# A float32 decoder trunk on one core: in the gate and up product, two of eight pairs of feature tiles are multiplied blockwise with seven products (Strassen's scheme) instead of eight

## The chip, the core and the metric

The kernel runs on one core of a Trainium2 chip. The core has TensorE (matrix products, called PE in the profile; its weight loads, PEld, are listed apart and overlap the products), VectorE (DVE), ScalarE (ACT), GpSimd (POOL) and SyncE (SP, which here only issues transfers). The metric is the device time of one execution in microseconds (us).

## The reference, cut to what matters

One sequence of 256 tokens with 2048 features goes through two layers: dilated attention and then attention over a shared latent K/V, each followed by this feed-forward part with 5632 hidden features:

```python
def swiglu(xn, w_gu, w_down):
    g, u = jnp.split(xn @ w_gu, 2, axis=-1)
    return (jax.nn.silu(g) * u) @ w_down

h = h + swiglu(rms_norm(h, ffn_norm_g[layer]), ffn_w_gu[layer], ffn_w_down[layer])
```

`xn` is 256 x 2048, `w_gu` is 2048 x 11264 (gate columns, then up columns), `w_down` is 5632 x 2048. Everything is float32.

## The kernel before, in words

**Precision.** A float32 operand is split into two parts, `hi` (rounded to the format that TensorE multiplies in one pass, fp32r) and `lo` (the rest). A product of two such operands is three matmuls, hi·hi, hi·lo and lo·hi, added up in PSUM (lines 416 to 418). So one 128-token tile by one 128 x 512 weight block costs three matmuls of 512 columns.

**Weights.** All weights come as units of 128 partitions x 2048 values, in one list made in advance. `WeightStream` (lines 84 to 158) loads a unit from HBM into one of four `raw` buffers (line 100, on SP's queue), and splits it in two halves of 1024: ACT copies `hi` (line 141), DVE subtracts to get `lo` (line 142). `hi` and `lo` have three buffers each (`ahead + 1`), so the split of a unit can begin when PE is done with the unit three before it, two units ahead of its use. A `raw` buffer is free for the next load when its split is done.

**Feed-forward** (`ffn`, line 585). The 44 hidden tiles are worked off in 11 blocks of four (512 hidden columns), in three parts of 4, 4 and 3 blocks (`FFN_PARTS`); after each part its share of the down product is added to `h`. A block runs `product` twice: four units of gate weights (each four feature tiles by 512 columns), then four of up weights, with `xT` (the normalized input, feature-major, hi and lo, 16 feature tiles) stationary and the weights moving. Each `product` has an accumulator `acc` of two PSUM banks (two token tiles by 512); there are two such accumulators, so gate and up alternate. ACT applies Silu with the row scale `rstd` from PSUM (line 595), DVE multiplies the up product from PSUM (line 598). After the first unit of the next block PE transposes the result (line 351), and ACT and DVE split it into `hT` (lines 326, 327). The second factor `rstd` is applied where the down product is added to `h` (line 603).

**Order.** A scheduler orders each engine's instructions at build time: by readiness in its own model of the times, and by program order among ready ones. On the chip each engine then runs its list in that order. `Later` (put and tick) places deferred pieces of work in program order after so many units. `across` (line 376) spreads a per-token scale over a row with a small matmul. The four single banks of PSUM (`bank`, line 198) serve transposes and attention.

Of the kernel before, what the change touches and what calls it, by code (L numbers as in the profile page):

```python
# [10 lines left out]
F32 = mybir.dt.float32  # L11
F32R = mybir.dt.float32r
AF = mybir.ActivationFunctionType
# [29 lines left out]
C_ID, C_M0, C_M1, C_M2, C_MB = 0, 128, 640, 896, 1152  # L43
C_CA, C_SA, C_CB, C_SB, C_END = 1536, 1792, 2048, 2304, 2560
# [38 lines left out]
class WeightStream:  # L83
# [4 lines left out]
    def __init__(self, nc, raw_pool, hl_pool, units, raw_bufs, ahead):  # L88
        self.nc, self.raw_pool, self.hl_pool, self.units = nc, raw_pool, hl_pool, units
        self.raw_bufs, self.ahead = raw_bufs, ahead  # L90
        self.raws, self.parts = {}, {}
        self.n_raw = self.n_split = self.at = 0

    def load(self, upto):
        while self.n_raw < min(upto, len(self.units)):
            ap = self.units[self.n_raw][0]
            _, nk, ncol = ap.shape
            t = self.raw_pool.tile([P, 2048], F32, tag="raw", name="raw", bufs=self.raw_bufs)
# [27 lines left out]
    def split(self, upto):  # L126
        nc = self.nc
        while self.n_split < min(upto, len(self.units)):
            self.load(self.n_split + 1)
            raw = self.raws.pop(self.n_split)  # L130
            _, gain, form = self.units[self.n_split]
            _, nk, ncol = raw.shape
# [15 lines left out]
            self.n_split += 1  # L148

# [30 lines left out]
def kernel(ctx, tc, consts, x, attn_norm_g, ffn_norm_g, a_w_qkv, a_w_o, kv_norm_g,  # L180
# [7 lines left out]
    rawp = ctx.enter_context(tc.tile_pool(name="rawp", bufs=4))  # L188
# [47 lines left out]
    def load_rest():  # L236

        nc.sync.dma_start(out=cst, in_=consts[:, P:])
# [40 lines left out]
    def units_ffn(layer):  # L279
        for k0, n in FFN_PARTS:  # L280
            for j in range(k0, k0 + n, 4):
                for base in (0, FF):
                    for k in range(0, KD, 4):
                        add_unit(ffn_w_gu[layer], k, 4, base + j * P, 512)
# [18 lines left out]
    ws = WeightStream(nc, rawp, hlp, units, raw_bufs=4, ahead=2)  # L303
# [10 lines left out]
    cst = cpool.tile([P, C_END - P], F32, name="cst")  # L314
    later.put(3, load_rest)
    con = lambda at, n, rows=P: cst[:rows, at - P:at - P + n]
    cos_a, sin_a = con(C_CA, S, A_ROT), con(C_SA, S, A_ROT)
# [144 lines left out]
    def keys_first(blocks):  # L462
# [5 lines left out]
        pt = tmp.tile([P, 512], F32, tag="pt", name="pt")  # L468
# [22 lines left out]
    with tc.tile_pool(name="attn_a", bufs=2) as ap:  # L491

# [26 lines left out]
        def values_a(head, sm, vs):  # L519
            hs = slice(head % 4 * P, (head % 4 + 1) * P)  # L520
            p0 = keys_first([sm[:, t, a * P:(a + 1) * P] for a in range(NT) for t in range(NT)])
            p12 = keys_first([sm[:, t, o:o + P] for o in (S, S + P) for t in range(NT)])
# [62 lines left out]
    def ffn(xT, rstd, finish):  # L585

        with tc.tile_pool(name="ffn", bufs=3) as fp:
            for part, (k0, n) in enumerate(FFN_PARTS):
                last = part == len(FFN_PARTS) - 1
                hT = big_tile([P, 16, 2 * S], F32R, "hT")  # L590
                for j in range(0, n, 4):
                    hid = fp.tile([P, NT, 512], F32, tag="hid", name="hid")
                    acc = product(x_stationary, xT, KD)
                    for t in range(NT):
                        nc.scalar.activation(out=hid[:, t, :], in_=acc[:, t, :], func=AF.Silu,
                                             scale=rstd[:, t:t + 1])
                    acc = product(x_stationary, xT, KD)
                    nc.vector.tensor_tensor(out=hid, in0=acc, in1=hid, op=ALU.mult)
                    later.put(1, lambda j=j, hid=hid, hT=hT:
                              transposed([hid[:, t, :] for t in range(NT)], hT, j, None))  # L600
# [42 lines left out]
    with tc.tile_pool(name="attn_b", bufs=2) as bp:  # L643
# [60 lines left out]
        def values_b(head, sm, v):  # L704
            hs = slice(head % 2 * P, (head % 2 + 1) * P)
            pt = keys_first([sm[:, a:a + P] for a in (0, P, 2 * P)])
# [103 lines left out]
```

## Time and profile before

| | |
|---|---|
| median of 3 runs | 2710.32 us (2710.01 to 2710.9) |
| the profiled execution, its own time | 2711.3 us |
| its span, first to last instruction | 2709.5 us |
| PE, PEld, DVE, ACT busy in the span | 100%, 84%, 56%, 43% |
| granted TensorE clock, mean | 0.998 |
| moved from HBM | 491.57 MB, 182 GB/s |

Busy times of PE overlap one another (a matmul is recorded with its fill and drain), so the step from one matmul's start to the next is its price, not its recorded duration. `x8` at the end of a timeline row means that eight neighbours are merged into it. The release of a wait is named in brackets.

### The profile page before, as it was taken

To read this page: it belongs to the slowest core of one execution; us is meant where nothing else is said; L and a number is where in the kernel's file an instruction comes from. 1 tells how busy PE (TensorE), PEld (TensorE's weight loads), DVE (VectorE), ACT (ScalarE), POOL (GpSimd) and SP (SyncE) were. 2 spreads that over 40 slices of the span, in tenths; PEclk is the share of its full clock that TensorE was granted. 3 is DMA by queue.
4 is the path that set the end of the run, shared out by engine and by line. 5 is a ranking of instruction groups with operands and counts; after the bars stand their busy time and mean duration, and the time that the engine had idled before them with its cause. 6 is when DMAs were issued, how large, how long until landed. Compare 5 with 4: busy or idle time off the path is not lost.

```text
span 2709.5 us, 31962 instructions
## 1 busy us (share of the span) xinstructions
PE 2696.2 (100%) x13162; PEld 2272.5 (84%) x13162; DVE 1524.4 (56%) x2080; ACT 1164.0 (43%) x1517; POOL 5.5 (0%) x12
## 2 busy tenths in 40 slices
PE   9999999999999999999999999999999999999998
PEld 7888888888888888888888888888888888888887
DVE  5666576577476654454445445588554454445445
ACT  5444444443434444433443344565444433443443
POOL 0000000000000000000000000000000000000000
PEclk9999999999999999999999999999999999999999
DMA  7544555555554555655555555444555565556563
GB/s 284 187 163 164 187 170 171 186 172 171 175 183 161 197 187 188 195 191 189 190 195 187 193 184 192 146 152 138 185 186 187 189 199 186 189 191 195 186 209 118
DMA packets 299746, 495.73 MB, mean 183 GB/s; under 512 B 9848, under 2 KB 112976, under 8 KB 299088
## 3 DMA queue, kind: packets, MB, share of 16 engines
q1 hardware_dynamic: 298976, 492.63, 55.5%
q8 instruction: 103, 1.69, 0.2%
q10 hardware_dynamic: 624, 1.07, 0.1%
q14 instruction: 43, 0.35, 0.0%
HBM read 491.57 MB, written 2.10 MB: 182 GB/s over the span
## 4 chain that ended last, share of the span: by engine, by line
PE 98%; DVE 1%; ACT 0%; issue 0%; DMA 0%; SPq 0%; POOL 0%; POOLq 0%; DVEq 0%; ACTq 0%
PE acc L417 24%; PE acc L418 24%; PE acc L416 24%; PE acc L397 14%; PE acc L400 7%; PE bank L351 1%; PE bank L510 1%; PE bank L467 1%; PE bank L525 1%; PE bank L529 1%; PE bank L698 0%; PE bank L697 0%; PE bank L708 0%; DVE lo L142 0%; DMA xt<-in_x_dram 0%
## 5 line engine op out<-in xcount | busy, mean ns | idle before, releaser
L142 DVE TENSOR_TENSOR lo<-raw,hi 128x1024 fp32r<-128x1024 f32 (+2 forms) x930 | 1083.9, 1195 | 965.0 <-ACT hi L141 949.2
L141 ACT CAST hi<-raw 128x1024 fp32r<-128x1024 f32 (+2 forms) x930 | 915.9, 1030 | 1283.7 <-PE acc L418 874.0
L416 PE MATMUL acc<-hi,xT_f 128*128 128x512 f32 x1408 | 549.3, 390 | 0.0
L418 PE MATMUL acc<-hi,xT_f 128*128 128x512 f32 x1408 | 548.0, 389 | 0.0
L417 PE MATMUL acc<-lo,xT_f 128*128 128x512 f32 x1408 | 547.9, 389 | 0.0
L397 PE MATMUL acc<-xT_a,hi 128*128 128x512 f32 x1536 | 379.5, 395 | 0.0
L397 PEld LDWEIGHTS acc<-xT_a,hi 128*128 128x128 f32 x1536 | 281.5, 188 | 53.9
L418 PEld LDWEIGHTS acc<-hi,xT_f 128*128 128x128 f32 x1408 | 264.4, 188 | 54.9
L417 PEld LDWEIGHTS acc<-lo,xT_f 128*128 128x128 f32 x1408 | 264.4, 188 | 54.3
L416 PEld LDWEIGHTS acc<-hi,xT_f 128*128 128x128 f32 x1408 | 264.4, 188 | 54.3
L416 PE MATMUL acc<-hi,hT 128*128 128x512 f32 x704 | 274.6, 390 | 0.0
L418 PE MATMUL acc<-hi,hT 128*128 128x512 f32 x704 | 274.0, 389 | 0.0
L417 PE MATMUL acc<-lo,hT 128*128 128x512 f32 x704 | 273.9, 389 | 0.0
L400 PEld LDWEIGHTS acc<-xT_a,lo 128*128 128x128 f32 x1536 | 196.9, 191 | 7.6
L400 PE MATMUL acc<-xT_a,lo 128*128 128x256 f32 x1536 | 199.1, 283 | 0.0
L417 PEld LDWEIGHTS acc<-lo,hT 128*128 128x128 f32 x704 | 132.2, 188 | 27.3
L418 PEld LDWEIGHTS acc<-hi,hT 128*128 128x128 f32 x704 | 132.2, 188 | 27.3
L416 PEld LDWEIGHTS acc<-hi,hT 128*128 128x128 f32 x704 | 132.2, 188 | 27.1
L416 PE MATMUL acc<-hi,xT_a 128*128 128x512 f32 x384 | 151.1, 393 | 0.0
L417 PE MATMUL acc<-lo,xT_a 128*128 128x512 f32 x384 | 150.4, 392 | 0.6 <-DVE lo L142 0.6
L418 PE MATMUL acc<-hi,xT_a 128*128 128x512 f32 x384 | 150.8, 393 | 0.0
L417 PEld LDWEIGHTS acc<-lo,xT_a 128*128 128x128 f32 x384 | 72.4, 188 | 15.7 <-DVE lo L142 1.3
(171 smaller groups left out, 2073.3 us busy)
## 6 DMA issues: line engine op xcount, KB each, us to landing
raw<-in_ffn_w_gu_dram SPq DMA_DIRECT2D x176, 1024.0 KB, 5.0
raw<-in_a_w_qkv_dram SPq DMA_DIRECT2D x143, 1024.0 KB, 4.9
raw<-in_ffn_w_down_dram SPq DMA_DIRECT2D x88, 1024.0 KB, 5.0
raw<-in_a_w_o_dram SPq DMA_DIRECT2D x16, 1024.0 KB, 5.1
raw<-in_b_w_o_dram SPq DMA_DIRECT2D x16, 1024.0 KB, 5.1
raw<-in_b_w_kv_b_dram SPq DMA_DIRECT2D x8, 1024.0 KB, 5.3
raw<-in_b_w_q_b_dram SPq DMA_DIRECT2D x8, 768.0 KB, 4.5
raw<-in_b_w_q_a_dram SPq DMA_DIRECT2D x4, 1024.0 KB, 5.1
```

The costliest lines, as they stand in the source:

```text
L141: nc.scalar.copy(out=h, in_=src)
L142: nc.vector.tensor_tensor(out=l, in0=src, in1=h.bitcast(F32), op=ALU.subtract)
L351: nc.tensor.transpose(out=ps[:, jj * S + t * P:jj * S + (t + 1) * P], in_=srcs[t][:, (j + jj) * P:(j + jj + 1) * P], identity=ident)
L397: mm(out=acc[:, i, :], lhsT=sl(hi, kk), rhs=xT[:, k0 + kk, :], start=first and kk == 0, stop=False)
L400: mm(out=acc[:, i, 0:S], lhsT=sl(lo, kk), rhs=xT[:, k0 + kk, 0:S], start=False, stop=last and kk == nk - 1)
L416: mm(out=acc[:, t, :ncol], lhsT=xh, rhs=rhs(hi, kk), start=st, stop=False)
L417: mm(out=acc[:, t, :ncol], lhsT=xh, rhs=rhs(lo, kk), start=False, stop=False)
L418: mm(out=acc[:, t, :ncol], lhsT=xl, rhs=rhs(hi, kk), start=False, stop=sp)
L467: nc.tensor.transpose(out=ps[:, i * P:(i + 1) * P], in_=b, identity=ident)
L510: mm(out=ps[:, t * n:(t + 1) * n], lhsT=q[:, hh, qt], rhs=kt[:, hh, ks], start=True, stop=True)
L525: mm(out=ot[:, :S], lhsT=vs[0][:, a, hs], rhs=p0[:, a * S:(a + 1) * S], start=a == 0, stop=False)
L529: mm(out=ot[:, t * P:(t + 1) * P], lhsT=vs[g][:, t, hs], rhs=p12[:, o:o + P], start=False, stop=(g, t) == (2, NT - 1))
```

## The change

In blocks 1 to 10 of each layer's feed-forward (all but the first), two of the eight pairs of feature tiles (pairs 2 and 5, `SEVEN`) are multiplied by Winograd's form of Strassen's scheme. The 2 x 2 blocks are: two token tiles by two feature tiles of `xT`, times two feature tiles by (up, gate) columns of the weights. Seven block products replace eight; each is still three matmuls.

What else it takes:
- A unit of `w_gu` now holds two feature tiles of both up and gate, [up k, gate k, up k+1, gate k+1] by 512 columns. It is loaded by two transfers of 512 KB. A block still has eight units, and gate and up are accumulated side by side over all eight, in the two accumulators at once (`ga`, `ua`).
- A unit of a pair in `SEVEN` is split into `hi`, `lo` for three of its four blocks (1536 columns), then four subtractions and additions of 512 columns on DVE form the four weight sums in place in `raw`, and these are split into `th`, `tl` (one buffer each) in two halves of 1024.
- The token sums are formed once per layer from the scaled `xT` (`scaled`, `forms`): `xT` is multiplied in place by the power of two in `rstd` (eight DVE instructions of 1024 columns per layer, as the first block's units are done), and the rest of `rstd`, `rem`, is applied in the block's end; the factor in the down product's `add` goes.
- Four of the seven products have single PSUM banks of their own (`pb`, all four banks) that stay open from pair 2 to pair 5. After pair 5, one ACT copy and four DVE additions of 512 columns combine them; at the block's end two DVE additions of 1024 columns add `ga` and `ua`, and two of 512 per token tile apply Silu's factor.
- There are three `raw` buffers instead of four, and part of the constants and the tile `pt` move into the pool of the first attention.

The diff, cut:

```diff
+SEVEN = (2, 5)
...
+            ap, _, form = self.units[self.n_raw]
+            t = self.raw_pool.tile([P, 2048], F32, tag="raw", name="raw", bufs=self.raw_bufs)
+            if form in ("eight", "seven"):
+                v = t.rearrange("p (k n c) -> p k n c", n=2, c=512)
+                for n in range(2):
+                    self.nc.sync.dma_start(out=v[:, :, 1 - n, :], in_=ap[n])
...
+    def halve(self, hi, lo, src):
+        self.nc.scalar.copy(out=hi, in_=src)
+        self.nc.vector.tensor_tensor(out=lo, in0=src, in1=hi.bitcast(F32), op=ALU.subtract)
+
+    def split_blocks(self, raw, form):
...
+        hi, lo = [self.hl_pool.tile([P, 2048], F32R, tag=n, name=n, bufs=self.ahead + 1) for n in ("hi", "lo")]
+        if form == "eight":
+            for i in (slice(0, 1024), slice(1024, 2048)):
+                self.halve(hi[:, i], lo[:, i], raw[:, i])
+            return hi, lo
+        i = slice(512, 2048)
+        self.halve(hi[:, i], lo[:, i], raw[:, i])
+        th, tl = [self.sum_pool.tile([P, 2048], F32R, tag=n, name=n, bufs=1) for n in ("th", "tl")]
+        b12, b11, b22, b21 = [blk(raw, j) for j in range(4)]
+        tt = self.nc.vector.tensor_tensor
+        tt(out=b22, in0=b22, in1=b12, op=ALU.subtract)
+        tt(out=b12, in0=b12, in1=b11, op=ALU.subtract)
+        tt(out=b11, in0=b11, in1=b22, op=ALU.add)
+        tt(out=b21, in0=b21, in1=b11, op=ALU.subtract)
+        for i in (slice(0, 1024), slice(1024, 2048)):
+            self.halve(th[:, i], tl[:, i], raw[:, i])
+        return hi, lo, th, tl
...
-    ws = WeightStream(nc, rawp, hlp, units, raw_bufs=4, ahead=2)
+    ws = WeightStream(nc, rawp, hlp, units, raw_bufs=3, ahead=2)
...
+            later.put(1, lambda: row.update(R=across(r2, "R")))
...
+            def scaled(kp):
+                x2 = xT[:, 2 * kp:2 * kp + 2, :].rearrange("p k (h s) -> p k h s", s=S)
+                nc.vector.tensor_tensor(out=x2, in0=x2.bitcast(F32), in1=by, op=ALU.mult)
...
+            def mixed(seven, gate, up):
+                ga, ua = acc_tile(), acc_tile()
...
+                for kp in range(KD // 2):
+                    w = ws.next()
...
+                    if seven and kp in SEVEN:
...
+                            pb = [bank() for _ in range(4)]
...
+                        mul(pb[0], x(0, 0), w[:2], 1, st, sp)
+                        mul(ga[:, 0], x(0, 1), w[:2], 3, False, False)
+                        mul(ua[:, 0], y(3), w[:2], 2, False, False)
+                        mul(ga[:, 1], x(1, 1), w[2:], 3, False, False)
+                        mul(pb[1], y(0), w[2:], 0, st, sp)
+                        mul(pb[2], y(1), w[2:], 1, st, sp)
+                        mul(pb[3], y(2), w[2:], 2, st, sp)
+                    else:
+                        st, sp = kp == 0, kp == KD // 2 - 1
+                        for acc, n in ((ga, 1), (ua, 0)):
+                            for t in range(NT):
+                                mul(acc[:, t], x(t, 0), w, n, st, False)
+                                mul(acc[:, t], x(t, 1), w, n + 2, False, sp)
+                    later.tick()
+                    if seven and kp == SEVEN[-1]:
+                        u2 = fp.tile([P, 512], F32, tag="u2", name="u2")
+                        nc.scalar.copy(out=gate[:, 0], in_=pb[0])
+                        for o, x_, y_ in ((u2, pb[2], gate[:, 0]), (gate[:, 1], pb[3], u2),
+                                          (up[:, 0], pb[1], u2), (up[:, 1], pb[1], gate[:, 1])):
+                            nc.vector.tensor_tensor(out=o, in0=x_, in1=y_, op=ALU.add)
+                for acc, d in ((ga, gate), (ua, up)):
+                    nc.vector.tensor_tensor(out=d, in0=acc, in1=d, op=ALU.add)
...
+                    for t in range(NT):
+                        nc.scalar.activation(out=gate[:, t], in_=g[:, t], func=AF.Silu, scale=sc_[:, t:t + 1])
+                    for t in range(NT):
+                        nc.vector.scalar_tensor_tensor(out=up[:, t], in0=u[:, t], scalar=sc_[:, t:t + 1],
+                                                       in1=gate[:, t], op0=ALU.mult, op1=ALU.mult)
...
-                    nc.vector.scalar_tensor_tensor(out=chunk(t, c), in0=acc[:, t, :], scalar=rstd[:, t:t + 1],
-                                                   in1=chunk(t, c), op0=ALU.mult, op1=ALU.add)
+                    nc.vector.tensor_tensor(out=chunk(t, c), in0=acc[:, t, :], in1=chunk(t, c), op=ALU.add)
```

## Rows read from the trace of the kernel before

**Rows 1.** The page's busy time of each engine over the span, and of its 40 slices the DVE and the granted clock.

```profile
PE 2696.2 (100%) x13162; PEld 2272.5 (84%) x13162; DVE 1524.4 (56%) x2080; ACT 1164.0 (43%) x1517; POOL 5.5 (0%) x12
...
DVE  5666576577476654454445445588554454445445
...
PEclk9999999999999999999999999999999999999999
```

**Rows 2.** The page's chain of work that ended last, by engine and by line.

```profile
PE 98%; DVE 1%; ACT 0%; issue 0%; DMA 0%; SPq 0%; POOL 0%; POOLq 0%; DVEq 0%; ACTq 0%
PE acc L417 24%; PE acc L418 24%; PE acc L416 24%; PE acc L397 14%; PE acc L400 7%; PE bank L351 1%; PE bank L510 1%; PE bank L467 1%; PE bank L525 1%; PE bank L529 1%; PE bank L698 0%; PE bank L697 0%; PE bank L708 0%; DVE lo L142 0%; DMA xt<-in_x_dram 0%
```

**Rows 3.** The groups of gate and up matmuls, shapes kept apart: count, busy us, mean ns, idle before.

```profile
L416 PE MATMUL acc<-hi,xT_f 128*128 128x512 f32 x1408 | 549.3, 390 | 0.0
L418 PE MATMUL acc<-hi,xT_f 128*128 128x512 f32 x1408 | 548.0, 389 | 0.0
L417 PE MATMUL acc<-lo,xT_f 128*128 128x512 f32 x1408 | 547.9, 389 | 0.0
```

**Rows 4.** The timeline of PE in one block (start, us): the first matmul of two neighbouring units, the transposes, and the first two matmuls after them.

```profile
1105.18 0.39 PE L416 MATMUL acc<-hi,xT_f 128*128 128x512 f32 x1
...
1110.62 0.39 PE L416 MATMUL acc<-hi,xT_f 128*128 128x512 f32 x1
...
1116.07 1.03 PE L351 MATMUL bank<-ident,hid 128*128 128x128 f32 x8
1116.86 0.48 PE L416 MATMUL acc<-hi,xT_f 128*128 128x512 f32 x1
1117.17 0.39 PE L417 MATMUL acc<-lo,xT_f 128*128 128x512 f32 x1
```

**Rows 5.** The timeline of ACT and DVE for the split that runs while PE works on the unit begun at 1105.18.

```profile
1105.38 2.00 ACT L141 CAST hi<-raw 128x1024 fp32r<-128x1024 f32 x2 [3.43 <-PE acc L418]
...
1106.47 2.36 DVE L142 TENSOR_TENSOR lo<-raw,hi 128x1024 fp32r<-128x1024 f32 x2 [3.08 <-ACT hi L141]
```

**Rows 6.** Groups of DVE and ACT instructions over the span, shapes kept apart, for their mean ns.

```profile
L142 DVE TENSOR_TENSOR lo<-raw,hi 128x1024 fp32r<-128x1024 f32 x894 | 1064.4, 1220 | 965.0 <-ACT hi L141 949.2 <-PE acc L400 15.6
L141 ACT CAST hi<-raw 128x1024 fp32r<-128x1024 f32 x894 | 899.4, 1050 | 1278.9 <-PE acc L418 874.0 <-PE acc L397 288.1 <-issue 95.2
...
L435 ACT COPY t<-acc 128x512 f32<-128x512 f32 x64 | 37.6, 588 | 10.5 <-PE acc L400 10.5
...
L603 DVE SCALAR_TENSOR_TENSOR h<-acc,rstd,h 128x512 f32<-128x512 f32 x48 | 33.9, 747 | 53.0 <-PE acc L418 53.0
L436 DVE TENSOR_TENSOR qk<-acc,t 128x512 f32<-128x512 f32 x48 | 32.9, 685 | 0.0
...
L327 DVE TENSOR_TENSOR hT<-bank,hT 128x512 fp32r<-128x512 f32 x44 | 28.2, 684 | 0.0
...
L595 ACT ACTIVATE hid<-acc,rstd 128x512 f32<-128x512 f32 x44 | 27.9, 686 | 68.7 <-PE acc L418 68.7
L598 DVE TENSOR_TENSOR hid<-acc,hid 128x1024 f32<-128x1024 f32 x22 | 26.9, 1225 | 43.9 <-PE acc L418 43.9
...
L326 ACT CAST hT<-bank 128x512 fp32r<-128x512 f32 x44 | 23.5, 587 | 0.0
...
L389 DVE TENSOR_TENSOR qk<-qk,R 128x512 f32<-128x512 f32 x24 | 16.4, 685 | 0.0
...
L142 DVE TENSOR_TENSOR lo<-raw,hi 128x512 fp32r<-128x512 f32 x20 | 13.1, 686 | 0.0
...
L141 ACT CAST hi<-raw 128x512 fp32r<-128x512 f32 x20 | 11.6, 622 | 4.8 <-DMA raw<-in_a_w_qkv_dram 4.7
```

**Rows 7.** Busy time of each engine in two whole blocks of the first feed-forward, from 1024.5 to 1111.0 us.

```profile
1024.50:1111.00 86.50, 86.50 (x391) 71.82 (x390) 40.08 (x37) 34.49 (x39) 0.00 (x0) 1.00 0.57 185
```

**Rows 8.** The timeline at the one place where `across` runs between matmuls of the same kind, behind eight transposes.

```profile
1714.46 1.03 PE L351 MATMUL bank<-ident,h 128*128 128x128 f32 x8
...
1715.34 0.60 PE L383 MATMUL bank<-diag,ones 128*128 128x256 f32 x2
...
1715.58 0.58 PE L416 MATMUL acc<-hi,xT_b 128*128 128x512 f32 x1
...
1716.00 0.40 PE L417 MATMUL acc<-lo,xT_b 128*128 128x512 f32 x1
```

**Rows 9.** The chain to `rstd` before the first feed-forward, on DVE and POOL, and PE's transposes beside it.

```profile
981.39 0.70 POOL L366 TENSOR_TENSOR rstd<-rsq_v,mhalf 128x2 f32<-128x2 f32 x1 [955.13 <-DVE rsq_v L365]
982.79 1.03 PE L351 MATMUL bank<-ident,h 128*128 128x128 f32 x8
```

**Rows 10.** Transfers: issues by tensor, KB each, median us from issue to landing.

```profile
raw<-in_ffn_w_gu_dram SPq DMA_DIRECT2D x176, 1024.0 KB, 5.0
...
xt<-in_x_dram SPq DMA_DIRECT2D x3, 512.0 KB, 9.7
```

**Rows 11.** Whom SP's queue waited for: us in total, times, longest.

```profile
SPq L100 <- DVE lo L142: 2244.4, 425, 9.7
```

**Rows 12.** The first 27 us: length, busy us of PE, PEld, DVE, ACT, POOL, granted clock, DMA share, GB/s.

```profile
0.00:27.00 27.00, 24.19 (x110) 20.04 (x111) 16.43 (x40) 19.12 (x39) 0.91 (x5) 0.94 0.93 332
```

**Rows 13.** The timeline of DVE and ACT in the start: the splits of the second unit's last quarter and the third unit, and of the fifth unit's first half.

```profile
15.88 0.69 DVE L142 TENSOR_TENSOR lo<-raw,hi 128x512 fp32r<-128x512 f32 x1
16.83 2.36 DVE L142 TENSOR_TENSOR lo<-raw,hi 128x1024 fp32r<-128x1024 f32 x2 [0.25 <-ACT hi L141]
...
24.78 1.04 ACT L141 CAST hi<-raw 128x1024 fp32r<-128x1024 f32 x1
```

More of the change, by code (lines that the diff above doesn't have):

```diff
@@ L131, in split @@
             _, gain, form = self.units[self.n_split]
+            if form in ("eight", "seven"):
+                self.parts[self.n_split] = self.split_blocks(raw, form)
+                self.n_split += 1
+                continue
             _, nk, ncol = raw.shape
@@ L280, in units_ffn @@
         for k0, n in FFN_PARTS:
+            v = ffn_w_gu[layer].rearrange("(k p) c -> p k c", p=P)
             for j in range(k0, k0 + n, 4):
-                for base in (0, FF):
-                    for k in range(0, KD, 4):
-                        add_unit(ffn_w_gu[layer], k, 4, base + j * P, 512)
+                for kp in range(KD // 2):
+                    blocks = [v[:, 2 * kp:2 * kp + 2, b + j * P:b + j * P + 512] for b in (0, FF)]
+                    units.append((blocks, None, "seven" if j > 0 and kp in SEVEN else "eight"))
             for c in range(0, D, 512):
@@ L312, with con @@
         ws.load(i + 1)
-    cst = cpool.tile([P, C_END - P], F32, name="cst")
+    cst, cst_a = cpool.tile([P, C_M0 - C_MB], F32, name="cst"), []
     later.put(3, load_rest)
-    con = lambda at, n, rows=P: cst[:rows, at - P:at - P + n]
-    cos_a, sin_a = con(C_CA, S, A_ROT), con(C_SA, S, A_ROT)
+    def con(at, n, rows=P):
+        t, base = (cst, C_MB) if at < C_M0 else (cst_a[0], C_M0)
+        return t[:rows, at - base:at - base + n]
     cos_b, sin_b = con(C_CB, S), con(C_SB, S)
@@ L591, in ffn @@
                 for j in range(0, n, 4):
-                    hid = fp.tile([P, NT, 512], F32, tag="hid", name="hid")
-                    acc = product(x_stationary, xT, KD)
-                    for t in range(NT):
[L595 to L600, printed above, removed]
+                    gate, up = [fp.tile([P, NT, 512], F32, tag=m, name=m) for m in ("gate", "up")]
+                    first = k0 + j == 0
+                    if first:
+                        for kp in range(KD // 2):
+                            later.put(kp + 3, lambda kp=kp: scaled(kp))
+                    g, u = mixed(not first, gate, up)
+                    sc_ = rstd if first else rem
+                    for t in range(NT):
+                        nc.scalar.activation(out=gate[:, t], in_=g[:, t], func=AF.Silu, scale=sc_[:, t:t + 1])
+                    for t in range(NT):
+                        nc.vector.scalar_tensor_tensor(out=up[:, t], in0=u[:, t], scalar=sc_[:, t:t + 1],
+                                                       in1=gate[:, t], op0=ALU.mult, op1=ALU.mult)
+                    later.put(1, lambda j=j, up=up, hT=hT:
+                              transposed([up[:, t, :] for t in range(NT)], hT, j, None))
                 def add(acc, c, t):
-                    nc.vector.scalar_tensor_tensor(out=chunk(t, c), in0=acc[:, t, :], scalar=rstd[:, t:t + 1],
-                                                   in1=chunk(t, c), op0=ALU.mult, op1=ALU.add)
+                    nc.vector.tensor_tensor(out=chunk(t, c), in0=acc[:, t, :], in1=chunk(t, c), op=ALU.add)
                     if last:
```

68 lines of the change are left out of this document (55 added, 13 removed).

## The prediction

> **What bounds the kernel now.** I read the busy times first, then the chain of work that ended last, then PE's groups and timeline, then what stands beside it. PE is busy in all of the span, DVE in 56%, ACT in 43% [rows 1], and 98% of the chain is PE, 72% of it the three matmul lines 416 to 418 [rows 2]. The 4224 gate and up matmuls show no idle time before them [rows 3]. So a matmul that goes is worth its step, as long as nothing else comes late. The step: two neighbouring units of 24 matmuls start at 1105.18 and 1110.62, so 5.44 / 24 = 0.2267 us for 512 columns [rows 4] (not the recorded 0.39, which overlaps), at a granted clock of 1.00, the upper of the two levels (2.4 GHz) [rows 7]. Eight transposes cost 1116.86 - 1116.07 = 0.79 us [rows 4].
>
> **What goes.** Each unit of a pair in `SEVEN` has 21 matmuls instead of 24. Two such units in 10 blocks of 2 layers: 40 x 3 = 120 matmuls less, 120 x 0.2267 = 27.2 us. A page of the Trainium skill prices this lower: "TensorE: Matmul & The Clock Gate" (Back-to-back issue gap) gives 512 columns at the upper clock about 216 ns, by which the saving would be 25.9 us. The row's step holds here, since it is measured on these very matmuls.
>
> **What PE gets in addition.** One `across` per layer. Where it runs now, transposes start at 1714.46 and should end 0.79 later, at 1715.25; the second matmul behind it starts at 1716.00, where 1117.17 - 1116.86 = 0.31 would be due without it [rows 4, 8]: 0.44 us each, 0.9 in all. Its input is ready in time: `rstd` leaves POOL at 981.39 + 0.70 = 982.1, one small DVE step and two for the diagonal follow (under 1 us), while PE transposes from 982.79 to 983.58 [rows 9]. I put this wait at 0, at most 1 us per layer.
>
> **What DVE and ACT get.** Durations by shape [rows 6]: DVE subtraction 0.69 (512) and 1.22 (1024), so 1.75 for 1536, at most 1.91 if paid as 512 plus 1024; DVE with an operand in PSUM 0.685 (512), 1.225 (1024); with a scalar 0.75; ACT copies 0.62 and 1.05, so 1.48 for 1536; from PSUM 0.59, Silu 0.69. A seven-unit costs DVE 1.75 + 4 x 0.685 + 2 x 1.22 = 6.9 and ACT 1.48 + 2 x 1.05 = 3.6, while its matmuls last 21 x 0.2267 = 4.76. An eight-unit costs DVE 2.44 and ACT 2.1 against 5.44. A block then has on DVE 6 x 2.44 + 2 x 6.9 + 4 x 0.685 (combine) + 2 x 1.225 (`ga`, `ua`) + 2 x 0.75 + 2 x 0.68 (`hT`) = 36.6 us, on ACT 12.6 + 7.2 + 0.6 + 1.4 + 1.2 = 23 us, against PE's 186 x 0.2267 + 0.79 = 42.95. Today it is 20.0 and 17.2 of 43.3 in a window of two blocks, halved [rows 7] (22.1 for DVE by the same durations). DVE goes from under a half to 85% but stays below PE, so this sum costs nothing on average; what it can cost is lateness, so the order inside a block decides.
>
> **A block, walked through.** Let 0 be its first matmul. Pair 1 starts at 6.23 (5.44 and the transposes), pair 2 at 11.67, 3 at 16.43, 4 at 21.87, 5 at 27.31, 6 at 32.07, 7 at 37.51; the next block at 42.95. Now a split starts 0.2 us after PE leaves the unit three before, DVE follows 1.09 later and the unit is ready 3.65 after the start [rows 5], 7 us early.
> - Pair 2: its split may start at 0. From 0 DVE owes `ua`'s addition 1.23, Silu's factor 1.5, the 1536 columns 1.75, four sums 2.74, `hT` 1.37, `tl` 2.44: 11.0 us. `hi` and `lo` are needed at 11.67, `th` and `tl` only after nine matmuls, at 13.7. 2.7 us are left, enough for two waits of 1.09 on ACT.
> - Pair 5: its split starts at 16.43, needs 1.09 + 1.75 + 2.74 and then the halves, 8.9 alone, with 2.4 for pair 6's split mixed in 11.3; ready at 27.8 at the latest, needed (`th`) at 29.35.
> - `pb` is combined from 31.4 on, the last three additions after 32.07, done by 35; nobody waits before 37.5.
> - The block's end: `ga` and `ua` are both in use, so the next block's first matmul waits until DVE has read `ga`. In pair 7 `ga`'s matmuls come first, so it is complete 12 x 0.2267 = 2.7 before the end. DVE is then in pair 1's split (of the next block), which ends about 1.8 before the end (3.65 after the unit's start) [rows 5]; the addition takes 1.225 and ends 0.6 before PE needs it. `ua` is needed 2.7 later still. I put this at 0 to 0.1 us per block, so 1 us in all with the other waits.
> - The first block of a layer gets `scaled`, eight times 1.22 and twice some 2.5 for the forms, in units where DVE has only 2.44 of 5.44: hidden, 0; without cover at most 15 us per layer.
> - The down product's add has no scalar any more, 0.685 instead of 0.75: off the path except for the last, under 0.1.
>
> **Loads.** A gate and up unit comes in two transfers of 512 KB; a unit lands 5.0 us after issue [rows 10]. SP's queue waits for DVE 425 times [rows 11]: each load is issued the moment a buffer is free. With four buffers it lands some 13 us before its split, with three 7.6 (the split three units on starts 3 x 5.44 later, less 3.65 and 5.0). Behind a waiting load on SP stand the next loads, the constants and the first attention's input. At the start DMA runs at 0.93 of its share, 332 GB/s [rows 12]: the fifth unit would be issued when the second's split ends (16.6), and land by about 22, before its split at 24.78 [rows 13]. I put three buffers at 0, between -2 (the last part of `xt` no longer queued behind a weight load) and +5 (one transfer's time).
>
> **The sum.** 2711.3 - 27.2 + 0.9 + 1.0 = 2686.0 for the profiled execution, which stands 1.0 above the median; so 2685 for the median, 0.93% less.
>
> **Rivals.**
> 1. *The single accumulator pair.* If in the static order another DVE instruction of 1024 columns stands ahead of `ga`'s addition, or DVE runs behind there, the 0.6 us of slack is gone: 1.22 - 0.6 = 0.6 us at each of 20 block ends, 13 us, 2698; at 1.3 us per block end (26 / 20) the saving is lost. For it: two accumulators are all there are, and now both are in use at once. Against it: the order in the trace puts a ready product before the splits that follow it. "Perfetto Trace Analysis" of the Trainium skill (Optimization Strategy) says that a gap repeated on the engine that should be busy can mean too little SBUF or PSUM for the next tile; this would be such a gap, and no row of before shows one.
> 2. *The load behind the sums, ending slower.* The sums are formed in `raw` itself, so a seven-unit's buffer is free only when `tl` is done, about 11 after the block's start for pair 2; then the load for pair 5 takes 5.0 and lands at 16.0 to 16.5, exactly when its split may begin. If it takes the 9.7 us that 512 KB take behind other transfers [rows 10], pair 5's split runs from 20.7 to 32.0 with the mixing above, 2.6 past its need, 52 us over 20 blocks: 2711 - 26 + 52, about 2737. It turns the change into a loss from 1.3 us per block on, that is from a landing of about 8.4 us. Against it: the 9.7 are from the start, where DMA stands at 0.93 of its share; here it is 0.57 [rows 7].
> 3. *Three buffers elsewhere.* In the attention stages DVE is at 0.7 to 0.8 in some slices [rows 1], splits come late, and the missing buffer may cost some thirty loads 0.3 us each, 10 us: 2695.
>
> **Chances.** The forecast 0.64 (2682 to 2690); rival 1 0.18, of which 0.05 would fall within the measurement's bound; rival 2 0.11; rival 3 0.07. About 0.2% (5.4 us) is what a measurement of this kernel can tell from no change. Faster by more: 0.64 + 0.13 + 0.07 = 0.84; within: 0.05; slower: 0.11. The range takes in the forecast's lower bound (start -2, no waits: 2681) and rivals 3 and most of 1: 2681 to 2703.
>
> **What would show it.** Right: 13162 - 120 + 4 matmuls; the step of 0.2267 unchanged; blocks of 43.0 us instead of 44.3; DVE at some 36 us per block, busy about 1840 us in all (1524 + 20 x (36.6 - 22.1) + 2 x 15); no repeated idle time of PE in front of seven-units or block starts. Wrong: PE waiting for `ga`'s addition at the block's first matmul (rival 1), for `tl` in pair 5 with ACT's first copy of that unit released by a DMA (rival 2), or a longer span before 970 us, where nothing but the buffers changed (rival 3).

## The result, and the profile after

The changed kernel takes 2688.11 us (median of four runs, 2687.61 to 2689.08) against 2710.61 (four runs, 2710.01 to 2711.02): ratio 0.9918, 95% interval 0.99 to 0.9935. It is 22.5 us faster, 3.1 us slower than forecast, and inside the range. The profiled execution took 2688.55 us, its span 2686.7.

The page after, for [rows 1] and [rows 2]: busy time of each engine, the DVE's 40 slices, and the chain of work that ended last.

```profile
PE 2672.7 (99%) x13046; PEld 2249.9 (84%) x13046; DVE 1824.8 (68%) x2472; ACT 1231.4 (46%) x1581; POOL 5.5 (0%) x12
...
DVE  5676576477477668756785686588577747874875
...
PE 98%; DVE 1%; ACT 1%; issue 0%; DMA 0%; SPq 0%; POOL 0%; POOLq 0%; DVEq 0%; ACTq 0%
```

PE has the 13046 matmuls foretold and is still the whole chain; the 300 us more on DVE lie beside it. One whole block of the first feed-forward, for [rows 7] (length; busy us of PE, PEld, DVE, ACT, POOL; granted clock, DMA share, GB/s):

```profile
1027.90:1071.14 43.24, 43.24 (x197) 35.74 (x196) 34.62 (x37) 21.45 (x24) 0.00 (x0) 1.00 0.56 195
```

The window of [rows 7] is 86.50 us long, while two blocks of before are 88.86, so it is not quite two whole blocks and its halves are too small: in one whole block of before, DVE is busy 21.2 and ACT 18.2 of 44.43.

To find where the time went, both spans are cut at four starts: the first matmul that reads `xT_f`, the first that reads `xT_b`, the first that reads the second layer's `xT_f`, and the last matmul of all, where the tail begins. Lengths in us; "block" is the distance of the first transposes of two neighbouring blocks. The other kernels of this study stand in the same table, as differences to before, to be read with their experiments.

| kernel | time | start | feed-forward 1 | attention between | feed-forward 2 | tail | block |
|---|---|---|---|---|---|---|---|
| before | 2710.61 | 977.34 | 731.68 | 263.23 | 728.73 | 8.55 | 44.43 |
| **after** | 2688.11 | -0.84 | -11.13 | -0.06 | -11.13 | +0.36 | 43.24 |
| no pair | 2711.03 | -1.93 | +0.75 | -0.18 | +0.75 | +0.35 | 44.43 |
| one pair | 2699.52 | -1.41 | -5.19 | -0.08 | -5.19 | +0.08 | 43.83 |
| before, three `raw` | 2710.21 | -1.06 | 0 | -0.05 | 0 | +0.01 | 44.43 |
| no `forms` | 2690.24 | -0.39 | -10.46 | -0.15 | -10.46 | +0.36 | 43.31 |
| no open banks | 2687.11 | -1.90 | -11.13 | -0.10 | -11.13 | +0.06 | 43.24 |
| hi, lo only | 2684.98 | -0.66 | -12.85 | -0.06 | -12.85 | +0.07 | 43.07 |
| `ga` last | 2696.29 | -1.27 | -6.83 | -0.09 | -6.91 | +0.07 | 43.24 |
| both late | 2715.01 | -1.27 | +2.44 | -0.10 | +2.45 | +0.08 | 44.23 |
| two `raw` | 2730.75 | +5.14 | +7.97 | -0.94 | +7.20 | +0.07 | 43.6 to 47.8 |
| pairs 1, 3, 5 | 2685.55 | -0.64 | -12.87 | -0.09 | -12.25 | +0.09 | mostly 42.7 to 43.4 |
| pairs 1, 4, 6 | 2686.66 | -1.40 | -12.73 | -0.07 | -11.31 | +0.10 | mostly 42.67 or 43.25 |
| 1, 3, 5, sums on POOL | 2753.57 | -0.95 | +22.99 | -0.07 | +21.49 | +0.46 | 44.6 to 46.8 |

All of it came from the blocks: every one of the 20 is 44.43 - 43.24 = 1.19 us shorter. Ten are 11.87 per layer; 11.13 arrived, so 0.74 is lost elsewhere in each. Both parts of that are in the timeline. First `across`, for [rows 8]:

```profile
981.95 1.03 PE L398 MATMUL bank<-ident,h 128*128 128x128 f32 x8
982.82 0.60 PE L430 MATMUL bank<-diag,ones 128*128 128x256 f32 x2
983.07 0.58 PE L675 MATMUL acc<-hi,xT_f 128*128 128x512 f32 x1
983.49 0.40 PE L676 MATMUL acc<-lo,xT_f 128*128 128x512 f32 x1
```

983.49 - 981.95 is 1.54 where 0.79 + 0.31 were due: 0.44, as taken, and no wait for `rstd`. The other 0.3 is the one wait of PE inside the feed-forward, once per layer, at the end of the first block: both accumulators are in use there too, and ACT's Silu must read one before PE can go on. The waits (us in total, times, longest):

```profile
PEld acc L675 <- ACT gate L726: 0.8, 2, 0.4
```

### The profile page after: what moved, and what is told of

Read it like the earlier page. It is cut to its first block, busy times and chain, and to the rows that moved or that the text cites. A ratio compares the mean times of both kernels' runs of the same rounds, so it can differ in the third digit from the quotient of the medians.

```text
span 2686.7 us, 32652 instructions
## 1 busy us (share of the span) xinstructions
PE 2672.7 (99%) x13046; PEld 2249.9 (84%) x13046; DVE 1824.8 (68%) x2472; ACT 1231.4 (46%) x1581; POOL 5.5 (0%) x12
## 4 chain that ended last, share of the span: by engine, by line
PE 98%; DVE 1%; ACT 1%; issue 0%; DMA 0%; SPq 0%; POOL 0%; POOLq 0%; DVEq 0%; ACTq 0%
PE acc L444 14%; PE acc L464 12%; PE acc L465 12%; PE acc L463 12%; PE acc L675 10%; PE acc L677 10%; PE acc L676 10%; PE acc L447 7%; PE bank L676 1%; PE bank L675 1%; PE bank L677 1%; PE bank L398 1%; PE bank L559 1%; PE bank L514 1%; PE bank L574 1%; PE bank L578 1%
## 5 line engine op out<-in xcount | busy, mean ns | idle before, releaser
L157 DVE TENSOR_TENSOR lo<-raw,hi 128x1024 fp32r<-128x1024 f32 (+2 forms) x578 | 667.3, 1178 | 476.1 <-ACT hi L156 460.2
L156 ACT CAST hi<-raw 128x1024 fp32r<-128x1024 f32 (+2 forms) x578 | 561.3, 1016 | 758.4 <-PE acc L444 297.3
L167 DVE TENSOR_TENSOR lo<-raw,hi 128x1024 fp32r<-128x1024 f32 (+1 forms) x312 | 392.1, 1288 | 157.6 <-ACT hi L166 157.5
L166 ACT CAST hi<-raw 128x1024 fp32r<-128x1024 f32 (+1 forms) x312 | 333.1, 1104 | 346.0 <-issue 147.2
L675 PE MATMUL acc<-hi,xT_f 128*128 128x512 f32 x1128 | 441.3, 391 | 0.0
L676 PE MATMUL acc<-lo,xT_f 128*128 128x512 f32 x1128 | 439.5, 390 | 0.0
L677 PE MATMUL acc<-hi,xT_f 128*128 128x512 f32 x1128 | 439.5, 390 | 0.0
L675 PEld LDWEIGHTS acc<-hi,xT_f 128*128 128x128 f32 x1128 | 211.8, 188 | 44.7 <-ACT gate L726 0.8
L677 PEld LDWEIGHTS acc<-hi,xT_f 128*128 128x128 f32 x1128 | 211.8, 188 | 44.5
L676 PEld LDWEIGHTS acc<-lo,xT_f 128*128 128x128 f32 x1128 | 211.8, 188 | 43.8
L465 PE MATMUL acc<-hi,xT_a 128*128 128x512 f32 x384 | 150.9, 393 | 0.0
```

The lines of the kernel that those rows point to most:

```text
L156: nc.scalar.copy(out=h, in_=src)
L157: nc.vector.tensor_tensor(out=l, in0=src, in1=h.bitcast(F32), op=ALU.subtract)
L166: self.nc.scalar.copy(out=hi, in_=src)
L167: self.nc.vector.tensor_tensor(out=lo, in0=src, in1=hi.bitcast(F32), op=ALU.subtract)
L465: mm(out=acc[:, t, :ncol], lhsT=xl, rhs=rhs(hi, kk), start=False, stop=sp)
L675: mm(out=out, lhsT=xh, rhs=wh, start=st, stop=False)
```

## Did the walked block hold?

DVE around the start of the block at 1064.91:

```profile
1060.76 2.36 DVE L167 TENSOR_TENSOR lo<-raw,hi 128x1024 fp32r<-128x1024 f32 x2 [2.15 <-ACT hi L166]
1063.04 1.22 DVE L711 TENSOR_TENSOR gate<-acc,gate 128x1024 f32<-128x1024 f32 x1
1065.11 1.23 DVE L711 TENSOR_TENSOR up<-acc,up 128x1024 f32<-128x1024 f32 x1 [0.86 <-PE acc L677]
1066.44 1.42 DVE L728 SCALAR_TENSOR_TENSOR up<-up,rem,gate 128x512 f32<-128x512 f32 x2
1067.77 1.75 DVE L167 TENSOR_TENSOR lo<-raw,hi 128x1536 fp32r<-128x1536 f32 x1
1069.56 0.69 DVE L184 TENSOR_TENSOR raw<-raw 128x512 f32<-128x512 f32 x1
...
1074.08 2.35 DVE L167 TENSOR_TENSOR tl<-raw,th 128x1024 fp32r<-128x1024 f32 x2
```

The order is the one walked: the split of the next block's pair 1, then `ga`'s addition at once, ending at 1064.26, 0.65 before the block (foretold 0.6); then `ua`, Silu's factor, pair 2's split and sums. Its `tl` is done at 1076.43, 11.5 into the block (foretold 11.0). The first matmul that reads it starts at 1078.99, 2.6 later. For [rows 10, 11]: transfers (KB, median us from issue to landing), SP's waits for a `tl` in the unit's own loads, and ACT's first copy of pair 5.

```profile
raw<-in_ffn_w_gu_dram SPq DMA_DIRECT2D x352, 512.0 KB, 4.5
```

```profile
SPq L105 <- DVE tl L167: 357.8, 34, 12.3
```

```profile
1081.54 1.48 ACT L166 CAST hi<-raw 128x1536 fp32r<-128x1536 f32 x1 [2.60 <-DMA raw<-in_ffn_w_gu_dram]
```

Pair 5's split begins at 16.6, released by its load, which lands just then, as foretold. It costs nothing, because its `tl` is then done at 25.6 and read at 29.8.

So the mechanisms held, and still 0.17 us per block is missing: 192 steps of 0.22667 and the transposes make up a block of before, 44.43 - 43.52 = 0.91 for the transposes; six matmuls less leave 186 x 0.22667 + 0.91 = 43.07, not 43.24. That is 3.5 us in 20 blocks, and PE shows no wait. The steps themselves are longer. PE in pair 2's unit: the first of its matmuls that reads `forms`, and the first of the next unit, 15 steps on.

```profile
1034.83 0.39 PE L675 MATMUL acc<-hi,forms 128*128 128x512 f32 x1
...
1038.28 0.39 PE L675 MATMUL acc<-hi,xT_f 128*128 128x512 f32 x1
```

3.45 / 15 = 0.2300 at a granted clock of 1.00, with a weight load and a shape as in any other step.

## Experiments: what the rest of the change costs

Theory: the blocks' saving is proportional to the pairs, and apart from `across`, Silu's wait and the longer steps nothing of the change costs time. Rivals: a fixed price of the new unit layout and the paired accumulators (it would remain without pairs), or a price of DVE's load (it would grow from the first pair to the second).

**No pair.**

```diff
-SEVEN = (2, 5)
+SEVEN = ()
-                    g, u = mixed(not first, gate, up)
+                    g, u = mixed(False, gate, up)
```

(and `forms`, then empty, goes)

> The change with no pair multiplied by seven products: the new unit layout, gate and up side by side on both accumulators, the scaling of xT and three raw buffers stay. Theory A (the saving is the 120 matmuls less, reduced by longer steps inside the seven-units, and the rest of the change costs nearly nothing): blocks of 44.4 us as before, time before plus two across and the first block's wait on Silu (0.74 per layer) less 0.8 at the start, 2710 to 2712. Rival B (the 2.5 us that the saving fell short come from the rest of the change): 2713 to 2715, with blocks longer than 44.43.

2711.03 us beside 2710.76 for before. Blocks are 44.43, as before, though gate and up are accumulated side by side and each load comes in two transfers. What stays is 0.75 per layer, `across` and Silu's wait. So the new layout is free. (The additions at the block's end go with the pairs here, so this kernel says nothing of them.)

**One pair.**

```diff
-SEVEN = (2, 5)
+SEVEN = (2,)
```

> Only pair 2 by seven products. Theory A: per block 3 matmuls less (0.68) and half the longer steps (0.09), so 43.84 us a block and about 2700 in all, halfway between none and two. Rival B (a fixed cost of the rest): the first pair gains less than the second, blocks of 44.0 or more, 2702 to 2704.

2699.52. Blocks 43.83: the first pair takes 0.60, the second 0.59. Linear, while DVE is busy 30.2 us of a block here and 34.6 with two pairs: DVE's load costs nothing up to there.

**Three buffers alone**, in the kernel before.

```diff
-    ws = WeightStream(nc, rawp, hlp, units, raw_bufs=4, ahead=2)
+    ws = WeightStream(nc, rawp, hlp, units, raw_bufs=3, ahead=2)
```

(and `rawp` itself)

> The kernel before with three raw buffers instead of four, nothing else. Theory: the 0.84 us that the time up to the first feed-forward lost come from this, because the last part of xt is no longer queued behind the fourth weight load: span 0.8 us shorter, all of it in the first 30 us, 2709 to 2710. Rival 3 of the prediction (a buffer less costs time in the attention stages): longer by up to 10 us, with waits there.

2710.21. No stretch gets longer, so rival 3 falls. The start came out 0.4 to 1.9 us shorter in every kernel with three buffers; there is one trace of before, so it stays open how much of that is spread. Part of it goes with the clock: before ([rows 12], 0.94) and eight of the twelve kernels with three buffers have a stretch at a granted clock of 0.5, the lower of the two levels (1.2 GHz), in their first 14 us. The four without one (no pair, no open banks, both late, pairs 1, 4, 6) start 1.3 to 1.9 shorter, the eight others 0.4 to 1.4.

## Experiments: why the steps are longer

Three theories: PE is slowed by `forms` as stationary operand; by waits too short for the wait view, for the four open banks or for DVE; or by where it reads its operands, `forms`, `th` and `tl` in turn with `xT_f`, `hi` and `lo`. All three kernels leave out a part of the scheme, so their output is another.

**No `forms`.** The token sums are made, but PE reads slices of `xT_f` instead.

```diff
-                        y = lambda j: [forms[:, i, h, j, :] for h in range(2)]
+                        y = lambda j: x(j % 2, j // 2)
```

> The four products that take a token sum take a slice of xT instead (the sums are still formed; the output is another). Question: what makes the steps in a seven-unit 231 to 236 ns instead of 227, some 0.085 us per unit. Theory F (the change of the stationary operand between two tensors, xT and forms): steps are 227, blocks of 43.07 instead of 43.24, 2685. Theory W (the waits in the unit, seven in 21 matmuls, and the single banks): unchanged, 43.24, 2688.

2690.24 beside 2711.46 for before. Blocks 43.31: longer, not shorter. PE in pair 2's unit, from its first `th` on:

```profile
1035.95 0.40 PE L675 MATMUL acc<-th,xT_f 128*128 128x512 f32 x1
...
1038.05 0.40 PE L675 MATMUL bank<-th,xT_f 128*128 128x512 f32 x1
```

Nine steps in 2.10, 0.2333 each. `forms` is not the cause by itself.

**No open banks.** The four products go into `ga` and `ua`, their combination is left out, and the additions at the block's end become copies.

```diff
-                            pb = [bank() for _ in range(4)]
+                            pb = [ga[:, 0], ua[:, 0], ga[:, 1], ua[:, 1]]
...
-                    if seven and kp == SEVEN[-1]:
+                    if False:
...
-                    nc.vector.tensor_tensor(out=d, in0=acc, in1=d, op=ALU.add)
+                    nc.vector.tensor_copy(out=d, in_=acc)
```

> The four products with single banks of their own are added to ga and ua instead, and the combination after pair 5 is left out (the output is another); gate and up are copied out by DVE instructions of the same size as the additions. Theory W: five of the waits and the open banks are gone, so the steps in a seven-unit fall back towards 227, blocks of 43.07 to 43.15. Theory F: blocks stay at 43.24. In both, DVE loses 2.7 us a block and PE gains nothing by that, since DVE is off the path.

2687.11 beside 2711.46, blocks 43.24, with the same long steps (15 in 3.45):

```profile
1033.77 0.39 PE L675 MATMUL acc<-hi,forms 128*128 128x512 f32 x1
...
1037.22 0.39 PE L675 MATMUL acc<-hi,xT_f 128*128 128x512 f32 x1
```

So the open banks and the waits for them are not the cause. The waits for `th` and `tl` are still in this kernel.

**`hi` and `lo` only.** All work of ACT and DVE stays, but PE reads slices of `xT_f`, `hi` and `lo` where it read `forms`, `th` and `tl`.

```diff
-                        y = lambda j: [forms[:, i, h, j, :] for h in range(2)]
+                        y = lambda j: x(j % 2, j // 2)
...
-                        mul(ga[:, 1], x(1, 1), w[2:], 3, False, False)
-                        mul(pb[1], y(0), w[2:], 0, st, sp)
-                        mul(pb[2], y(1), w[2:], 1, st, sp)
-                        mul(pb[3], y(2), w[2:], 2, st, sp)
+                        mul(ga[:, 1], x(1, 1), w[:2], 3, False, False)
+                        mul(pb[1], y(0), w[:2], 1, st, sp)
+                        mul(pb[2], y(1), w[:2], 1, st, sp)
+                        mul(pb[3], y(2), w[:2], 2, st, sp)
```

> All seven products of a seven-unit take slices of xT as stationary and blocks of hi and lo as moving operand, in the same order, to the same accumulators and banks; forms, th and tl are still made, but PE does not read them (the output is another). Theory P (the longer steps come from where PE reads: forms, th and tl, in turn with xT and hi): steps 227, blocks of 43.05 to 43.10, 2685. Theory O (they come from the order of the products or of their outputs): steps of 231 to 236 stay, blocks 43.24 or more, 2688.

2684.98 beside 2711.22. The same 15 steps as above:

```profile
1035.00 0.39 PE L675 MATMUL acc<-hi,xT_f 128*128 128x512 f32 x1
...
1038.40 0.39 PE L675 MATMUL acc<-hi,xT_f 128*128 128x512 f32 x1
```

3.40 / 15 = 0.2267, and all 20 blocks are 43.07, just what six matmuls less should leave. So the cause lies in PE's reading of these tiles, worth 0.17 per block or 3.4 us. The waits for `th` and `tl` go with the reading, so this run does not part the two; but the long steps do not stand at the waits, as the changed kernel's PE shows at the end of pair 2's unit and after it:

```profile
1037.37 0.39 PE L677 MATMUL bank<-th,forms 128*128 128x512 f32 x1
...
1038.05 0.40 PE L677 MATMUL bank<-th,forms 128*128 128x512 f32 x1
1038.28 0.39 PE L675 MATMUL acc<-hi,xT_f 128*128 128x512 f32 x1
...
1039.44 0.39 PE L677 MATMUL acc<-hi,xT_f 128*128 128x512 f32 x1
```

Three steps that read nothing but `forms`, `th` and `tl` take 0.68, 0.227 each. Five steps in the next unit, which read only `xT_f`, `hi` and `lo` again, take 1.16, 0.232 each. Before has the same behind its transposes, without any of the new tiles: five steps of 0.232 from 1117.17 [rows 4] to this one:

```profile
1118.33 0.39 PE L416 MATMUL acc<-hi,xT_f 128*128 128x512 f32 x1
```

Whether it is the tiles' place in memory or the change from one tile to another is not settled, since no run separates the two; these rows speak for the change.

## Experiments: the two rivals with a price

**`ga` last.** Rival 1 says that the slack at the block's end hangs on `ga` being complete first. In the last unit the products of `ua` go first.

```diff
-                        for acc, n in ((ga, 1), (ua, 0)):
+                        for acc, n in (((ua, 0), (ga, 1)) if sp else ((ga, 1), (ua, 0))):
```

> In each block's last unit up's matmuls come before gate's, so that the accumulator that the next block needs first is finished last. Theory (one accumulator pair; the order in the last unit gives 2.7 us, of which 0.65 are left over): the addition of ga can start only 0.2 after the block's end and takes 1.22, so PE waits 1.4 us at 20 block ends and somewhat more (two Silu of 0.7) at two: about 2719 to 2723, and the whole saving is gone. Rival (the accumulators are not what is tight, another buffer serves): no change, 2688.

2696.29, and the blocks stay at 43.24: a miss. DVE at the end of a block:

```profile
1066.91 1.22 DVE L711 TENSOR_TENSOR up<-acc,up 128x1024 f32<-128x1024 f32 x1
1068.98 1.23 DVE L711 TENSOR_TENSOR gate<-acc,gate 128x1024 f32<-128x1024 f32 x1 [0.86 <-PE acc L677]
```

The scheduler puts `ua`'s addition first, and the next block's first accumulator must have got the buffer that `ua` had, since PE goes on while DVE still reads `ga`: names changed, and nothing else. Only the first block pays, +4.2 to +4.3 per layer, since there DVE reads `up` only behind Silu, and Silu's `gate` is now complete last. PE stands 2.7 us for it:

```profile
PE acc L675 <- ACT gate L726: 5.4, 2, 2.7
```

The other 1.6 us are the clock. Behind this gap, PE's step rises from 0.227 to 0.427 for seven matmuls, at a granted clock of 0.50, the lower level (columns as above):

```profile
1025.20:1028.50 3.30, 3.30 (x10) 2.53 (x9) 3.20 (x4) 0.00 (x0) 0.00 (x0) 0.50 0.00 0
```

```profile
1025.84 0.63 PE L676 MATMUL acc<-lo,xT_f 128*128 128x512 f32 x1
...
1027.97 0.63 PE L675 MATMUL acc<-hi,xT_f 128*128 128x512 f32 x1
```

**Both late.** To take the slack away for good, both accumulators must be complete only at the very end: in the last unit the products of its second feature tile go behind all the others, gate and up in turn.

```diff
+                                if not sp:
+                                    mul(acc[:, t], x(t, 1), w, n + 2, False, False)
+                        for t in range(NT if sp else 0):
+                            for acc, n in ((ga, 3), (ua, 2)):
+                                mul(acc[:, t], x(t, 1), w, n, False, True)
```

(for the line with `n + 2` of the loop as it was)

> Only the last unit of each block is reordered: the second feature tile's products come last, gate and up in turn, so that ga is complete 0.68 us and ua 0 us before the block's end, instead of 2.7 and 0. The buffer that is free first goes to the accumulator that the next block needs first, as the run with gate last showed. Theory (one pair of accumulators; 0.65 us of slack): ga's addition of 1.22 starts at about 0.5 before the end, so PE waits about 0.75 us at 20 block ends and 1 to 3 at two: blocks of 44.0, 2703 to 2709. Rival (the accumulators are not tight): 43.24, 2688.

2715.01 beside 2711.46: the whole saving is gone, with the number of matmuls unchanged. Blocks 44.23, +0.99 each instead of the 0.75 expected, and PE's waits name it, 20 block ends (14 with a block behind, six with a down product) and the two first blocks:

```profile
PEld acc L675 <- issue: 15.7, 14, 1.1
...
PE acc L675 <- DVE gate L715: 10.2, 14, 0.7
...
PE acc L463 <- DVE gate L715: 4.4, 6, 0.7
PE acc L675 <- ACT gate L730: 4.0, 2, 2.0
```

So rival 1 is real as a mechanism: 1.0 us per block end with all slack gone (the 0.6 of the prediction was for an addition one instruction late), and some 3.7 us at each first block (PE stands 2.0 for Silu, and the clock is at 0.50 behind it again). The changed kernel misses it by 0.65 us, and owes them to the order inside the last unit. "Perfetto Trace Analysis" of the Trainium skill (Optimization Strategy) says that a gap repeated on the engine that should be saturated can mean too little SBUF or PSUM for the next tile; here the trace agrees, with 14 such gaps of up to 0.7 at the block starts.

**Two `raw` buffers.** Rival 2 says that loads behind the in-place sums are the tight spot.

```diff
-    ws = WeightStream(nc, rawp, hlp, units, raw_bufs=3, ahead=2)
+    ws = WeightStream(nc, rawp, hlp, units, raw_bufs=2, ahead=2)
```

(and `rawp` itself)

> Two raw buffers instead of three. Theory (rival 2 of the prediction: the load behind the sums has nearly no slack with three; the trace of the change shows ACT waiting 51.7 us in 28 splits for gate and up loads, hidden by the two units of lead): one buffer less puts each load a unit later, pair 4's split 5 us and pair 5's 3 us late on top, so PE waits 1 to 4 us per block in the feed-forward, blocks of 44 to 47, and eight-units elsewhere lose little: 2710 to 2770. Rival (loads are far ahead): 2688 to 2690.

2730.75 beside 2711.22. The idle time of ACT that a load ended, 51.7 us in 28 waits in the changed kernel, grows, and PE waits for what comes late:

```profile
ACT hi L166 <- DMA raw<-in_ffn_w_gu_dram: 357.9, 117, 7.1
...
PEld acc L676 <- DVE lo L167: 9.0, 15, 1.0
...
PEld bank L676 <- DVE tl L167: 7.3, 21, 1.1
```

Blocks run from 43.6 to 47.8. The rival's place was right: in the changed kernel 18 of the 28 waits, 42.9 us, stand before pair 5's split, and with two buffers most of the time goes before those of pairs 4 and 7 (114.6 and 108.8 us), whose loads now come behind the sums of pairs 2 and 5. Three buffers are enough: one less costs 42.6 us, six of them in the start, and with three PE waits for no weights in the blocks.

## Experiments: can there be more pairs?

**Pairs 1, 3 and 5.**

```diff
-SEVEN = (2, 5)
+SEVEN = (1, 3, 5)
```

> Three pairs (1, 3, 5) by seven products. Theory A (PE is all that counts while DVE is below it): three more matmuls less, 0.59 us a block as for the first and the second pair, blocks of 42.65, 2676. Theory D (DVE becomes the bound): DVE has 34.7 + 7 = 41.6 us of work in 42.65, and what it waits for ACT and for loads no longer fits, so blocks are 43.2 or longer with PE waiting in front of seven-units, 2688 to 2710.

2685.55 beside 2711.46. That lies between the two theories. A third pair should give 0.59 more per block, 12 us; the two feed-forwards gained 2.9 over the changed kernel's. DVE is now busy 38.5 us of a block of 43.35, and PE stands for `th` and `tl` of pair 3:

```profile
PEld acc L676 <- DVE tl L167: 10.0, 18, 0.7
...
PEld acc L675 <- ACT th L166: 2.7, 6, 1.6
```

**The sums on GpSimd.** Its four sums per pair leave DVE, with the same three pairs.

```diff
-        tt = self.nc.vector.tensor_tensor
+        tt = self.nc.gpsimd.tensor_tensor
```

> Three pairs (1, 3, 5), and the four weight sums run on GpSimd instead of DVE. With three pairs and the sums on DVE blocks were 42.65 to 43.35, DVE busy 38.5 of 43.35, and PE waited for tl. Theory (DVE's queue delays tl): DVE loses 8.2 us a block, tl is in time, all blocks 42.65, 2676 to 2678. Rival (the chain of a seven-unit is what is long, and GpSimd, whose speed for such a sum no run has shown, makes it longer): PE waits for tl more than before, blocks of 43.5 or more, 2690 or more.

2753.57 (four runs, 2751.7 to 2757.5), ratio to before 1.0157, 1.014 to 1.0174: a clear loss, and not what relief for DVE would give. GpSimd, then DVE, in one stretch:

```profile
1033.92 1.29 POOL L185 TENSOR_TENSOR raw<-raw 128x512 f32<-128x512 f32 x1
1035.29 2.16 POOL L186 TENSOR_TENSOR raw<-raw 128x512 f32<-128x512 f32 x1
```

```profile
1034.04 2.26 DVE L167 TENSOR_TENSOR lo<-raw,hi 128x1024 fp32r<-128x1024 f32 x1 [0.36 <-ACT hi L166]
...
1036.22 2.31 DVE L167 TENSOR_TENSOR lo<-raw,hi 128x1024 fp32r<-128x1024 f32 x1
```

A sum takes GpSimd 1.29, or 2.16 when it begins behind a subtraction of DVE; it takes DVE 0.69. While GpSimd works, DVE's subtractions take 2.26 and 2.31 where they take 1.22 in the kernel before [rows 6]: the engines hold each other up. The Trainium skill states such a rule in "SBUF — State Buffer" (Who interferes with whom): a VectorE instruction with two inputs in SBUF and a GpSimd instruction that reads SBUF exclude one another. The trace agrees: the four instructions end in turn, at 1035.21, 1036.30, 1037.45 and 1038.53, the last three each some 1.1 us after the other engine's. So the sums and what stands behind them on DVE are late, and PE waits for both:

```profile
PEld bank L398 <- DVE up L728: 27.8, 28, 1.5
PEld acc L676 <- DVE tl L167: 25.9, 25, 1.1
```

**Pairs 1, 4 and 6**, to give DVE one more unit before the second pair.

```diff
-SEVEN = (2, 5)
+SEVEN = (1, 4, 6)
```

> Three pairs again, but pairs 1, 4 and 6 instead of 1, 3 and 5; nothing else is changed. Three pairs at 1, 3 and 5 gave blocks of 43.35 us in the middle of a part, where 43.24 less three matmuls at the longer step (0.593) would be 42.65; PE stood 0.7 us for th and tl of pair 3 (18 times, 10.0 us). Theory (lateness at one place): pair 3's sums queue on VectorE behind pair 1's sums and the additions of the block's end; with two units between the first and the second of the pairs VectorE has one more unit to catch up, the waits for tl go, blocks are 42.6 to 42.8, and the run is 8 to 11.9 us (20 x 0.593 at the most) shorter than the changed kernel's 2688: 2676 to 2680. Rival (load): with VectorE busy 38.5 of 43.35 us a third pair finds no room wherever it stands; the waits move to another pair or to the block's end, blocks stay at 43.1 to 43.4, and the run comes to 2684 to 2690.

2686.66 (four runs, 2685.89 to 2686.8), ratio to before 0.9911, 0.9894 to 0.9927; the interval of two pairs, 0.99 to 0.9935, overlaps this one. The waits for `tl` are gone, but the rival was right: they moved to the block's start.

```profile
PEld acc L675 <- issue: 10.3, 14, 1.0
...
PE acc L675 <- DVE gate L711: 4.8, 14, 0.6
```

DVE before such a start, and the block's first matmul:

```profile
1061.67 0.68 DVE L707 TENSOR_TENSOR up<-bank,gate 128x512 f32<-128x512 f32 x1
1062.27 0.68 DVE L185 TENSOR_TENSOR raw<-raw 128x512 f32<-128x512 f32 x1
1062.87 1.22 DVE L711 TENSOR_TENSOR gate<-acc,gate 128x1024 f32<-128x1024 f32 x1
```

```profile
1064.23 0.47 PE L675 MATMUL acc<-hi,xT_f 128*128 128x512 f32 x1 [0.33 <-DVE gate L711]
```

`ga`'s addition stands behind pair 6's combination and the next block's first sums, ends at 1064.09 and holds the block up; that is rival 1 at its point. In the first layer, blocks with the wait are 43.25, those without 42.67, the full gain of a third pair. To have it everywhere, some 0.6 us of DVE's work would have to go from ahead of `ga`'s addition; no run tries that. Neither version with three pairs is shown to beat two.

## Why the prediction was right, and by how much it missed

The forecast for the profiled execution was 2686.0, and 2688.55 came. Term by term, from the table:

| term | taken | measured |
|---|---|---|
| 120 matmuls less | -27.2 | -27.2, less 3.5 for longer steps: -23.7 |
| `across`, twice | +0.9 | +0.9 |
| small waits | +1.0 | +0.6 (Silu in the two first blocks), 0 elsewhere |
| three buffers, start | 0 (-2 to +5) | -0.8 |
| attention between, tail | 0 | +0.3 |
| sum | -25.3 | -22.7 |

- The step that failed is "the step of 0.2267 unchanged": a matmul that goes was worth 0.2267, but those that stayed in the seven-units became dearer, up to 0.236 for some twenty steps per unit, 0.085 us in all, and over 40 units that alone is more than the miss. I had taken the price of a step from eight-units, which read only `xT_f`, `hi` and `lo`, and had not asked what the new tiles do to it. Start, waits and tail came out 0.9 better together, and as far as that is the start it is luck.
- The saving is 0.2267 per matmul, as the kernel with `hi` and `lo` only shows: 44.43 - 43.07 = 1.36 for six. The 0.216 of the Trainium skill's "TensorE: Matmul & The Clock Gate" (Back-to-back issue gap) is that section's figure for a matmul by itself; for a stream of weight loads and matmuls it gives some 0.131, by which, as an estimate, 120 matmuls would be 15.7 us. This kernel agrees with neither. The changed kernel's time lies nearer to the sum by the page's 25.9, but for another reason.
- The block: 43.24, foretold 43.0 instead of 44.3. Both levels were low by 0.1, since I took the transposes at 0.79 and they cost 0.91, with the longer steps behind them (0.31 and then five of 0.232).
- DVE: 34.6 us per block instead of 36.6, and 1824.8 in all instead of 1840. Records of neighbouring instructions overlap (two subtractions of 1.22 are 2.35 together), which the sum of single durations missed. It cost nothing either way.
- Rival 1 was missed by 0.65 us of slack, rival 2 by 4.2 us at pair 5; rival 3 shows in no run: before with three buffers got longer in no stretch.
- Silu's wait in the first block was not foreseen. It lay within what was set aside.

## What to carry to other kernels

Where one engine is the chain, price a removed instruction by the step between starts, and then ask whether the instructions that remain keep theirs: they may read other tiles. Where double buffering is given up for the change, look for what now has to be complete first at the seam, and order the last unit for it; here that order is worth the whole saving. And walk one period by due times, not by mean load: DVE at 80% cost nothing, at 89% most of what the next pair brought.

## What the runs showed of the hardware

- A matmul of 512 columns steps at 0.2267 us with operands from `xT_f`, `hi` and `lo`, and at 0.230 to 0.233 on average where `forms`, `th` and `tl` come between, at the same granted clock, with no wait in the records. Five steps of 0.232 also follow eight transposes.
- A gap of PE can cost more than itself: behind 2.7 us in which PE stood, the granted clock was 0.50 from 1025.20 to 1028.50 and the step 0.427, 1.6 us more.
- GpSimd and DVE slow each other on sums in SBUF: GpSimd's 512 columns take 2.16 us instead of 1.29, DVE's subtraction of 1024 takes 2.26 to 2.31 instead of 1.22.
